# Head 0's keys and queries loaded earlier from a pool of their own, and the second layer's input transposed through more PSUM banks

## The chip, the cores and the metric

The kernel is one program for one core of a Trainium2 chip. Its engines are TensorE (PE, matmul; PEld is its weight load), VectorE (DVE), ScalarE (ACT), GpSimd (POOL) and SyncE (SP), which issues the DMAs here. Each engine works through its own list of instructions in order, so an instruction that waits holds up all behind it on that engine. The metric is the device time of one execution, in microseconds (us).

## The reference

Two layers over 512 latent tokens of width 2048, with 256 context tokens. Layer 1: modulated RMSNorm, one input projection, then a gated MLP (groups of 128 channels mixed over chunks of 128 tokens) and differential attention of 8 heads, concatenated, projected and added. Layer 2: modulated RMSNorm, projection into a, b and g, depthwise convolution of 31 taps, LayerNorm, gate, output projection.

```python
# even layer (layer 1)
q, k = diff_qk(bq, ...), diff_qk(bk, ...)      # RMSNorm per head, axial rotary on latents
p = softmax(q0 k0 / 8) - lam * softmax(q1 k1 / 8)
ob = p @ v                                     # keys and values: 512 latent + 256 context
ya = u * (w_s @ rms_norm(v) + b_s) * silu(ag)
yb = rms_norm(ob) * (1 - lambda_init) * silu(bg)
x1 = x + gt * (concat(ya, yb) @ w_out)
# odd layer (layer 2)
h2 = modulate(rms_norm(x1), shift, scale)
a, b, g = split(h2 @ w_in)
y = silu(layer_norm(conv31(a * sigmoid(b)))) * silu(g)
out = x1 + gt2 * (y @ w_out)
```

All is float32. The kernel splits each matmul operand into two reduced-precision parts, hi and lo, and adds three products, so a logical matmul is three matmul instructions.

## The kernel before

Weights stream from HBM in blocks of 1 MB (`load_w`): a DMA into one of three `raw` buffers (line 95), a cast on ScalarE to `whi` (line 103), a subtraction on VectorE or GpSimd to `wlo` (line 104); `whi` and `wlo` have two buffers each. The order of most work is set by a scheduler that models the time when the program is built; in the attention stage the order on TensorE is written out by hand (`manual_schedule`). Where a tile pool takes memory that an earlier pool has given back, the first use waits for the last users of that memory.

The stages that matter, in order of time:

- Queries, until about 478 us: `m_block` computes Q, `qk_post` normalises, rotates (tables `CG`, `SG`), transposes and splits it, and stores it to scratch in HBM (`q_s`, line 565). Pool group `p12a` closes behind it.
- AV, about 470 to 550 us: projection of the gating values, 4 weight blocks for each of two column halves. At its start SyncE loads the gating bias `bsb` and the mixing weights `wsr` (lines 654, 659). In each block's hook a block of another matrix (`raw<-in_o_ada_w_dram`) is loaded and added on VectorE into `acc` (lines 464, 466), for the second layer's modulation; these share the three `raw` buffers with the weights. VectorE also scales `bsb` (line 655).
- U, about 550 to 652 us: `t_group` for two groups of 4 column tiles, gating on VectorE (`mx`, line 711), stores to `ug_s`.
- Attention, 652 to about 970 us: pools `psS`, `psT`, `psO` and `at` open. For each head `load_kq` loads keys and queries in four DMAs: `kk` twice (384 KB each) and `qq` twice (512 KB each), all into 64 partitions; `load_v` loads values. TensorE fills its time with the projections of the two gates (`fill`, tiles `fm`), three matmuls a unit. It runs 24 units (FP), then `scores` of head 0's first query tile (`S`), 8 more units, then the rhythm of scores, transposes of weights, values and fill. `scores` writes one buffer `S` (3 banks); its maxima (line 855) and exponentials (line 865) must have read it before the next scores.
- Output projection and second layer's input, about 970 to 1190 us: `x1_done` and `x1_last` make x1, `make_h2` transposes it in halves of 256 tokens: for two k-tiles at a time, 4 matmuls with the identity into one bank `z` from `psM` (2 banks), then ScalarE writes `h2h` (line 1061) and VectorE `h2l` (line 1062). `t_half_steps` multiplies the halves with the first weights of the second layer (banks `a01` from `psA4`, 6 banks); after it come another `t_half` and the groups `tg`.
- The second layer, to the end: TensorE runs without gaps.

Of the kernel before, what the change touches and what calls it, by code (L numbers as in the profile page):

```python
# [11 lines left out]
F32 = mybir.dt.float32  # L12
F32R = mybir.dt.float32r
# [6 lines left out]
P = 128  # L20
D = 2048
KT = D // P
T = 512
# [3 lines left out]
TA = T + TC  # L27
# [3 lines left out]
DH = 64  # L31
# [14 lines left out]
def hybrid_layers_kernel(  # L46
# [7 lines left out]
    V, A, G, PE, SP = nc.vector, nc.scalar, nc.gpsimd, nc.tensor, nc.sync  # L54
# [7 lines left out]
    def nm(s):  # L62
        uid[0] += 1
        return f"{s}_{uid[0]}"

    def mm(o, l, r, start, stop):
        return PE.matmul(o, l, r, start=start, stop=stop)  # L67
# [7 lines left out]
    def htile(s, dt=F32R):  # L75
        return hp.tile([P, T], dt, tag="h", name=nm(s))

    def dscr(shape, s):
        return dr.tile(shape, F32, name=s, tag=s)
# [7 lines left out]
    q_s = dscr([H, 2, P, T], "q_s")  # L87
    k_s = dscr([H, 2, P, TA], "k_s")
# [26 lines left out]
    def t_group(W, c0, mov, pool, tag, ntile=4, nk=4, lo_eng=None, hook=None, prologue=None):  # L115
        ncols = ntile * P
        ps = [pool.tile([P, T], F32, tag=tag, name=nm("tg")) for _ in range(ntile)]
        for gi in range(KT // nk):
            hi, lo = load_w(W, gi * nk * P, nk, c0, ncols, lo_eng)
            for j in range(ntile):  # L120
                for k in range(nk):
                    kt = gi * nk + k
                    mh, ml = mov[kt]
                    wh, wl = hi[:, k, j * P : (j + 1) * P], lo[:, k, j * P : (j + 1) * P]
                    mm(ps[j], wh, mh, kt == 0, False)
                    mm(ps[j], wl, mh, False, False)
                    mm(ps[j], wh, ml, False, kt == KT - 1)
            if hook:
                hook(gi)
        return ps  # L130
# [95 lines left out]
    p123 = ctx.enter_context(ExitStack())  # L226
# [3 lines left out]
    def zt(n=T):  # L230
        return psM.tile([P, n], F32, tag="m", name=nm("z"))
# [415 lines left out]
    p12a.close()  # L647


    p12b = p12.enter_context(ExitStack())  # L650
    bp = p12b.enter_context(tc.tile_pool(name="bp", bufs=2))
    c2 = p12b.enter_context(tc.tile_pool(name="c2", bufs=1))
# [40 lines left out]
    for ug in range(2):  # L693
        ps = t_group(e_w_in, C_U + 512 * ug, hm, psA, "m", hook=u_hook if ug == 0 else hook2)
        for j in range(4):
            g = 4 * ug + j
            gu = bp.tile([P, T], F32, tag="gu", bufs=3, name=nm("gu"))
            A.activation(gu, ps[j], AF.Gelu)
            z = zt()
            for n in range(NT):  # L700
                o_ = z[:, n * P : (n + 1) * P]
                vh, vl = vn[n][0][:, g * P : (g + 1) * P], vn[n][1][:, g * P : (g + 1) * P]
                mm(o_, vh, wsh[:, g, :], True, False)
                mm(o_, vh, wsl[:, g, :], False, False)
                mm(o_, vl, wsh[:, g, :], False, True)
            z3 = z.rearrange("p (n q) -> p n q", q=P)
            V.scalar_tensor_tensor(
                z3, z3, gvh[:, g : g + 1], bsb[:, g, :].unsqueeze(1).broadcast_to([P, NT, P]), op0=ALU.mult, op1=ALU.add,
            )
            mx = bp.tile([P, T], F32, tag="mx", name=nm("mx"))  # L710
            V.tensor_tensor(mx, z, gu, op=ALU.mult)  # L711
            SP.dma_start(ug_s[g], mx)
    p12.close()


# [4 lines left out]
    at = p3.enter_context(tc.tile_pool(name="at", bufs=2))  # L720
# [96 lines left out]
    def fill(n):  # L817
        while n > 0 and not held:
            r = next(fs, None)
            if r != "more":  # L820
                held.append(r)
            n -= 1

    KQ, VV, S0, OT, PP = {}, {}, {}, {}, {}

    def load_kq(h):
        kk = at.tile([P, 2, TA], F32R, tag="kk", bufs=2, name=nm("kk"))
        qq = at.tile([P, 4, T], F32R, tag="qq", bufs=2, name=nm("qq"))
        for s in range(2):
            ds_ = slice(DH * s, DH * s + DH)  # L830
            SP.dma_start(kk[ds_].bitcast(F32), k_s[h, s].rearrange("(m d) t -> d m t", d=DH))
        for s in range(2):
            ds_ = slice(DH * s, DH * s + DH)
            SP.dma_start(qq[ds_].bitcast(F32), q_s[h].rearrange("s (m d) t -> d (s m) t", d=DH))
        KQ[h] = ([kk[:, m, :] for m in range(2)], [[qq[:, 2 * s + m, :] for s in range(2)] for m in range(2)])

    def load_v(h):
        vv = at.tile([P, 12, P], F32R, tag="vv", bufs=1, name=nm("vv"))
        SP.dma_start(vv.bitcast(F32), v_s[h].rearrange("s (k p) d -> p (s k) d", p=P))
        VV[h] = (vv[:, 0:6], vv[:, 6:12])  # L840
# [3 lines left out]
    def scores(h, qt):  # L844
        KK, QQ = KQ[h]
        if qt == 0:
            S0[h] = at.tile([P, NT], F32, tag="s0", name=nm("s0"))
        Sx = psS.tile([P, 2, TA], F32, tag="s", name=nm("S"))
        for m in (1, 0):
            for i, qx in enumerate(QQ[m]):  # L850
                for r0, r1 in (((0, 512), (512, 768)) if m == 0 else ((0, 256), (256, 768))):
                    mm(Sx[:, m, r0:r1], qx[:, qt * P : (qt + 1) * P], KK[m][:, r0:r1], i == 0, i == 1)
        mx = at.tile([P, 2], F32, tag="mx", name=nm("mx"))
        for m in (1, 0):
            V.reduce_max(mx[:, m : m + 1], Sx[:, m, :], axis=AX.X, negate=True)
        EX[h, qt] = (Sx, mx)
# [70 lines left out]

    with tc.manual_schedule(engines={mybir.EngineType.PE}):
        units = [(h, qt) for h in range(H) for qt in range(NT)]
        load_kq(0)  # L930
        load_v(0)
        fill(FP)
        scores(*units[0])
        weights(*units[0])
        fill(32 - FP)
        norm, outp = None, None
        for u, (h, qt) in enumerate(units):
            tail = u >= 4 * H - 4
            f0, f1, f2 = (2, 2, 2) if tail else (F0, F1, 8 - F0 - F1)
            if qt == 0 and h + 1 < H:  # L940
                load_kq(h + 1)
            if u + 1 < len(units):
                scores(*units[u + 1])
            fill(f0)
            turn(h, qt)
            if u + 1 < len(units):
                weights(*units[u + 1])
            fill(f1)
            if norm:
                outp = norm()  # L950
                norm = None
            if qt % 2:
                values(h, qt // 2)
                if outp:
                    outp()
                    outp = None
                if qt == 3:
                    norm = head_sums(h)
                    if h + 1 < H:
                        load_v(h + 1)  # L960
            fill(f2)
        outp = norm()
        fill(99)
        outp()
        for _ in fs:
            pass


    p3.close()
    psA = ctx.enter_context(tc.tile_pool(name="psA4", bufs=6, space=PSUM))  # L970
    rs4 = ctx.enter_context(tc.tile_pool(name="rs4", bufs=16))
    sg4 = ctx.enter_context(tc.tile_pool(name="sg4", bufs=12))
# [2 lines left out]
    def z4(n=T):  # L975
        return psM.tile([P, n], F32, tag="m", name=nm("z4"))

    def mt():
        return psA.tile([P, T], F32, tag="m", name=nm("m4"))
# [65 lines left out]

    def make_h2(half, kts):
        ts_ = slice(256 * half, 256 * half + 256)
        for k0 in range(kts[0], kts[1], 2):
            z = z4()
            for i in range(2):  # L1050
                for u in range(2):
                    kt, t = k0 + i, 2 * half + u
                    PE.transpose(z[:, 256 * i + u * P : 256 * i + (u + 1) * P],
                                 x1[t][kt // 4][:, (kt % 4) * P : (kt % 4 + 1) * P], ident)
            for i in range(2):
                kt = k0 + i
                if len(h2) <= kt:
                    h2.append((htile("h2h"), htile("h2l")))
                hi, lo = h2[kt]
                z_ = z[:, 256 * i : 256 * i + 256]  # L1060
                A.activation(hi[:, ts_], z_, AF.Identity, bias=sh2[:, kt : kt + 1])
                V.scalar_tensor_tensor(lo[:, ts_], z_, sh2[:, kt : kt + 1], hi[:, ts_].bitcast(F32), op0=ALU.add, op1=ALU.subtract)
# [39 lines left out]
    for t in range(2, NT):  # L1102
        part(t, 0)
    make_h2(0, (0, 8))
    for t in range(2, NT):
        part(t, 1)
        x1_last(t, ps[t][:, 0:256])
    make_h2(0, (8, 16))
    while ada_tail:
        ada_step(z4)  # L1110
# [112 lines left out]
    for i in range(KT):  # L1223
        if y2m[i] is None:
            z = z4()
# [61 lines left out]
```

## Time and profile before

| | |
|---|---|
| median of 3 runs | 1850.77 us (1850.75 to 1851.95) |
| profiled execution | 1853.68 us, span 1851.9 us |
| TensorE busy | 1805.9 us, 98% of the span, 8767 matmuls |
| VectorE busy | 1122.3 us (61%) |
| ScalarE busy | 559.8 us (30%) |
| GpSimd busy | 446.9 us (24%) |
| mean granted clock of TensorE | 0.996 of 2.4 GHz |
| DMA | 327.34 MB, mean 177 GB/s |

Read the span first, then the share of TensorE. It has little idle time, so what matters are the places where it waits or runs at the lower clock; the list of waits gives them, and the timelines of the engine that it waits for tell why. Lengths of matmuls in a timeline overlap, since they are pipelined: the distance between two starts is what one costs.

### The profile page before, as it was taken

How to read it: one execution, taken by the hardware profiler on the slowest of the kernel's cores; microseconds unless marked ns; L12 is line 12 of the kernel's file. 1: busy time of each engine (PE TensorE's matmuls, PEld its weight loads, DVE VectorE, ACT ScalarE, POOL GpSimd, SP SyncE). 2: the span in 40 equal slices, each digit the busy share in tenths (PEclk: the TensorE clock that was granted, in tenths of full speed). 3: DMA queues.
4: the chain of work that ended last, by engine and by line, in shares of the span. 5: the costliest groups of instructions: out<-in, count | busy, mean ns of one | idle time of the engine just before them, and what ended most of it. 6: DMA issues, size and time to landing. Idle time of an engine off the chain costs nothing.

```text
span 1851.9 us, 21931 instructions
## 1 busy us (share of the span) xinstructions
PE 1805.9 (98%) x8767; PEld 1475.8 (80%) x8767; DVE 1122.3 (61%) x1571; ACT 559.8 (30%) x747; POOL 446.9 (24%) x173
## 2 busy tenths in 40 slices
PE   5899999999999989999999999999999999999998
PEld 2557888888878878888888889888888888888887
DVE  4438546288556336666674555149999999765111
ACT  3322212222323124444442225322222222464120
POOL 0002002011000032232310002245445544444332
PEclk9999999999999999999999999999999999999999
DMA  9997764397767485655656772222332233224441
GB/s 312 360 333 254 245 240 123 118 347 232 241 230 240 165 225 161 170 164 167 203 193 228 250 232 86 91 91 91 102 103 91 91 104 101 91 91 142 149 158 52
DMA packets 208487, 327.34 MB, mean 177 GB/s; under 512 B 10249, under 2 KB 116610, under 8 KB 200194
## 3 DMA queue, kind: packets, MB, share of 16 engines
q1 hardware_dynamic: 208386, 325.94, 54.5%
q8 instruction: 69, 1.13, 0.3%
q14 instruction: 32, 0.26, 0.0%
HBM read 292.33 MB, written 33.58 MB: 176 GB/s over the span
## 4 chain that ended last, share of the span: by engine, by line
PE 83%; DMA 8%; DVE 4%; issue 2%; ACT 1%; POOL 1%; SPq 1%; DVEq 0%; ACTq 0%; POOLq 0%
PE tg L67 31%; PE mb L67 20%; PE m L67 14%; PE fm L67 8%; DMA raw<-in_o_ada_w_dram 3%; PE S L67 2%; PE oT L67 2%; PE z L305 2%; DVE wlo L104 2%; DVE acc L466 1%; DMA raw<-in_e_w_in_dram 1%; PE t L883 1%; DMA qq<-q_s 1%; DMA x_s<-x 1%; POOL wlo L104 1%
## 5 line engine op out<-in xcount | busy, mean ns | idle before, releaser
L104 POOL TENSOR_TENSOR wlo<-raw,whi 128x2048 fp32r<-128x2048 f32 x80 | 369.3, 4617 | 634.1 <-ACT whi L103 626.7
L103 ACT CAST whi<-raw 128x2048 fp32r<-128x2048 f32 x136 | 259.6, 1909 | 697.3 <-PE tg L67 209.7
L1152 DVE SCALAR_TENSOR_TENSOR z<-y,dwc,z 128x512 f32<-128x512 f32 x480 | 319.4, 749 | 0.1
L67 PE MATMUL tg<-h2h,wlo 128*128 128x512 f32 x704 | 274.7, 390 | 0.0
L67 PE MATMUL tg<-h2l,whi 128*128 128x512 f32 x704 | 273.9, 389 | 0.0
L67 PE MATMUL tg<-h2h,whi 128*128 128x512 f32 x704 | 270.8, 389 | 0.0
L67 PE MATMUL mb<-whi,hhi 128*128 128x512 f32 x512 | 203.0, 398 | 1.4 <-DVE ms L193 1.4
L67 PE MATMUL mb<-wlo,hhi 128*128 128x512 f32 x512 | 201.1, 393 | 1.5 <-DVE wlo L104 1.3
L104 DVE TENSOR_TENSOR wlo<-raw,whi 128x2048 fp32r<-128x2048 f32 x56 | 128.2, 2290 | 120.4 <-ACT whi L103 120.1
L67 PE MATMUL mb<-whi,hlo 128*128 128x512 f32 x512 | 200.9, 392 | 0.0
L466 DVE SCALAR_TENSOR_TENSOR acc<-raw,silu_c,acc 128x2048 f32<-128x2048 f32 x60 | 141.0, 2351 | 91.1 <-DMA raw<-in_o_ada_w_dram 70.2
L67 PEld LDWEIGHTS tg<-h2l,whi 128*128 128x128 f32 x704 | 132.2, 188 | 27.8 <-issue 0.5
L67 PEld LDWEIGHTS tg<-h2h,wlo 128*128 128x128 f32 x704 | 132.2, 188 | 27.7 <-issue 0.5
L67 PEld LDWEIGHTS tg<-h2h,whi 128*128 128x128 f32 x704 | 132.2, 188 | 27.5
L194 POOL TENSOR_TENSOR rs<-ms,mhalf 128x8 f32<-128x8 f32 x20 | 35.5, 1784 | 377.8 <-DVE ms L193 377.8
L67 PEld LDWEIGHTS mb<-whi,hhi 128*128 128x128 f32 x512 | 96.5, 189 | 34.6 <-issue 13.5
L67 PEld LDWEIGHTS mb<-wlo,hhi 128*128 128x128 f32 x512 | 96.7, 189 | 21.7 <-DVE wlo L104 2.7
L67 PEld LDWEIGHTS mb<-whi,hlo 128*128 128x128 f32 x512 | 96.6, 189 | 20.3
L67 PE MATMUL fm<-hhi,whi 128*128 128x512 f32 x256 | 106.7, 417 | 0.6 <-DVE mx L711 0.6
L67 PE MATMUL fm<-hlo,whi 128*128 128x512 f32 x256 | 101.1, 395 | 0.0
L67 PE MATMUL fm<-hhi,wlo 128*128 128x512 f32 x256 | 100.8, 394 | 0.0
L67 PE MATMUL m<-wlo,y2h 128*128 128x512 f32 x256 | 99.6, 389 | 0.0
(260 smaller groups left out, 3004.4 us busy)
## 6 DMA issues: line engine op xcount, KB each, us to landing
raw<-in_e_w_in_dram SPq DMA_DIRECT2D x56, 1024.0 KB, 6.4
raw<-in_o_ada_w_dram SPq DMA_DIRECT2D x48, 1024.0 KB, 5.0
raw<-in_o_w_in_dram SPq DMA_DIRECT2D x48, 1024.0 KB, 5.1
raw<-in_e_ada_w_dram SPq DMA_DIRECT2D x64, 512.0 KB, 7.2
raw<-in_e_ada_w_dram SPq DMA_DIRECT2D x16, 1024.0 KB, 6.7
raw<-in_e_w_out_dram SPq DMA_DIRECT2D x16, 1024.0 KB, 5.2
raw<-in_o_w_out_dram SPq DMA_DIRECT2D x16, 1024.0 KB, 5.0
qq<-q_s SPq DMA_DIRECT2D x16, 512.0 KB, 11.9
```

What stands on the lines that cost most here:

```text
L67: return PE.matmul(o, l, r, start=start, stop=stop)
L103: A.copy(hi, raw)
L104: (lo_eng or V).tensor_tensor(lo, raw, hi.bitcast(F32), op=ALU.subtract)
L194: G.tensor_tensor(dst, tmp, mhalf[:, 0:1].broadcast_to([P, n]), op=ALU.pow)
L305: PE.matmul(ada_ps[j][32 * g : 32 * g + 32, 0 : 2 * nc_], S[:, kt, :], raw[:, i, :], start=(kt < 4), stop=(kt >= KT - 4), skip_group_check ...
L466: V.scalar_tensor_tensor(ada_state["acc"], raw, sc_[:, jt : jt + 1], ada_state["acc"], op0=ALU.mult, op1=ALU.add)
L883: PE.transpose(z[:, k * P : (k + 1) * P], e[:, (k0 + k) * P : (k0 + k + 1) * P], ident)
L1152: V.scalar_tensor_tensor(zi if t == TAPS - 1 else z, y2[:, t : t + T], w(t), z, op0=ALU.mult, op1=ALU.add)
```

## The change

There are two edits. First, `load_kq` is defined before the AV stage and takes its tiles for even heads from a new pool `kq0`, opened where `p12a` has closed; odd heads use pool `at`, each with one buffer where `at` had two. Head 0's load is called after the first U group instead of at the start of attention. Second, `make_h2` takes every other transpose bank from `psA4` (`mt()`) instead of `psM` (`z4()`).

```diff
--- before.py
+++ after.py
@@ -647,6 +647,23 @@
     p12a.close()
 
 
+    pkq = p123.enter_context(ExitStack())
+    kq0 = pkq.enter_context(tc.tile_pool(name="kq0", bufs=1))
+    KQ = {}
+
+    def load_kq(h):
+        pool = at if h % 2 else kq0
+        kk = pool.tile([P, 2, TA], F32R, tag="kk", bufs=1, name=nm("kk"))
+        qq = pool.tile([P, 4, T], F32R, tag="qq", bufs=1, name=nm("qq"))
+        for s in range(2):
+            ds_ = slice(DH * s, DH * s + DH)
+            SP.dma_start(kk[ds_].bitcast(F32), k_s[h, s].rearrange("(m d) t -> d m t", d=DH))
+        for s in range(2):
+            ds_ = slice(DH * s, DH * s + DH)
+            SP.dma_start(qq[ds_].bitcast(F32), q_s[h].rearrange("s (m d) t -> d (s m) t", d=DH))
+        KQ[h] = ([kk[:, m, :] for m in range(2)], [[qq[:, 2 * s + m, :] for s in range(2)] for m in range(2)])
+
+
     p12b = p12.enter_context(ExitStack())
     bp = p12b.enter_context(tc.tile_pool(name="bp", bufs=2))
     c2 = p12b.enter_context(tc.tile_pool(name="c2", bufs=1))
@@ -710,6 +727,8 @@
             mx = bp.tile([P, T], F32, tag="mx", name=nm("mx"))
             V.tensor_tensor(mx, z, gu, op=ALU.mult)
             SP.dma_start(ug_s[g], mx)
+        if ug == 0:
+            load_kq(0)
     p12.close()
 
 
@@ -821,18 +840,7 @@
                 held.append(r)
             n -= 1
 
-    KQ, VV, S0, OT, PP = {}, {}, {}, {}, {}
-
-    def load_kq(h):
-        kk = at.tile([P, 2, TA], F32R, tag="kk", bufs=2, name=nm("kk"))
-        qq = at.tile([P, 4, T], F32R, tag="qq", bufs=2, name=nm("qq"))
-        for s in range(2):
-            ds_ = slice(DH * s, DH * s + DH)
-            SP.dma_start(kk[ds_].bitcast(F32), k_s[h, s].rearrange("(m d) t -> d m t", d=DH))
-        for s in range(2):
-            ds_ = slice(DH * s, DH * s + DH)
-            SP.dma_start(qq[ds_].bitcast(F32), q_s[h].rearrange("s (m d) t -> d (s m) t", d=DH))
-        KQ[h] = ([kk[:, m, :] for m in range(2)], [[qq[:, 2 * s + m, :] for s in range(2)] for m in range(2)])
+    VV, S0, OT, PP = {}, {}, {}, {}
 
     def load_v(h):
         vv = at.tile([P, 12, P], F32R, tag="vv", bufs=1, name=nm("vv"))
@@ -927,7 +935,6 @@
 
     with tc.manual_schedule(engines={mybir.EngineType.PE}):
         units = [(h, qt) for h in range(H) for qt in range(NT)]
-        load_kq(0)
         load_v(0)
         fill(FP)
         scores(*units[0])
@@ -967,6 +974,7 @@
 
 
     p3.close()
+    pkq.close()
     psA = ctx.enter_context(tc.tile_pool(name="psA4", bufs=6, space=PSUM))
     rs4 = ctx.enter_context(tc.tile_pool(name="rs4", bufs=16))
     sg4 = ctx.enter_context(tc.tile_pool(name="sg4", bufs=12))
@@ -1045,8 +1053,8 @@
 
     def make_h2(half, kts):
         ts_ = slice(256 * half, 256 * half + 256)
-        for k0 in range(kts[0], kts[1], 2):
-            z = z4()
+        for n, k0 in enumerate(range(kts[0], kts[1], 2)):
+            z = mt() if n % 2 else z4()
             for i in range(2):
                 for u in range(2):
                     kt, t = k0 + i, 2 * half + u
```

The scheduler decides where the instructions land. On SyncE, at the end of the query stores, the kernel before has these rows (`q_s` stores, then `bsb`, `wsr` and the streams of weights and modulation):

```order
L565 DMA q_s<-qklo_3350 128x4x128
L565 DMA q_s<-qkhi_3374 128x4x128
L95 DMA raw_3619<-in_e_w_in_dram 128x4x512
L565 DMA q_s<-qklo_3375 128x4x128
L565 DMA q_s<-qkhi_3399 128x4x128
L565 DMA q_s<-qklo_3400 128x4x128
L654 DMA bsb<-in_e_a_bs_dram 128x1024
L659 DMA wsr<-in_e_a_ws_dram 128x8x128
L95 DMA raw_3673<-in_o_ada_w_dram 128x2048
L95 DMA raw_3692<-in_e_w_in_dram 128x4x512
```

and the changed kernel these, in the same place:

```order
L565 DMA q_s<-qklo_3350 128x4x128
L660 DMA kk_4297<-k_s 64x2x768 x2
L663 DMA qq_4298<-q_s 64x4x512
L565 DMA q_s<-qkhi_3374 128x4x128
L663 DMA qq_4298<-q_s 64x4x512
L95 DMA raw_3622<-in_e_w_in_dram 128x4x512
L565 DMA q_s<-qklo_3375 128x4x128
L565 DMA q_s<-qkhi_3399 128x4x128
L565 DMA q_s<-qklo_3400 128x4x128
L671 DMA bsb<-in_e_a_bs_dram 128x1024
L676 DMA wsr<-in_e_a_ws_dram 128x8x128
L95 DMA raw_3676<-in_o_ada_w_dram 128x2048
```

Head 0's four loads (`kk` twice, `qq` twice) now stand among the query stores, ahead of the weight block `raw_3622` and of three stores; the rest keeps its order. At the start of attention, where they stood between the last weight block of the gates and `vv`, they are gone, and nothing else on SyncE has moved there.

On VectorE, at the start of the AV stage, the kernel before has

```order
L112 TENSOR_TENSOR qklo_3400<-z_3394,qkhi_3399 128x512
L655 TENSOR_SCALAR bsb<-bsb 128x1024
L104 TENSOR_TENSOR wlo_3622<-raw_3619,whi_3621 128x2048
L514 TENSOR_TENSOR A_96<-z_3546,o_b_92 128x16
L464 TENSOR_SCALAR acc_3555<-raw_3553,silu_c 128x2048
L516 TENSOR_TENSOR A_96<-A_96,g_89 128x16
L466 SCALAR_TENSOR_TENSOR acc_3555<-raw_3616,silu_c,acc_3555 128x2048
```

and the changed one

```order
L112 TENSOR_TENSOR qklo_3400<-z_3394,qkhi_3399 128x512
L104 TENSOR_TENSOR wlo_3625<-raw_3622,whi_3624 128x2048
L514 TENSOR_TENSOR A_96<-z_3549,o_b_92 128x16
L464 TENSOR_SCALAR acc_3558<-raw_3556,silu_c 128x2048
L672 TENSOR_SCALAR bsb<-bsb 128x1024
L516 TENSOR_TENSOR A_96<-A_96,g_89 128x16
L466 SCALAR_TENSOR_TENSOR acc_3558<-raw_3619,silu_c,acc_3558 128x2048
```

The scaling of `bsb` has moved behind the split of a weight block (`wlo`) and the first modulation step (`acc`). On TensorE, the transposes of x1 come in runs of up to 12 where they came in runs of up to 6, since four banks stand open at once instead of two; there are still 16 rounds of four, more of them early. At the end of the second half, where the next weights (`whi_9124`, accumulators `m_1485`, `m_1486`) begin, the kernel before has

```order
L67 MATMUL m_1468_8841<-h2l_8803,whi_8935 128x256
L67 MATMUL m_1469_8842<-h2l_8803,whi_8935 128x256
L67 MATMUL m_1485_9120<-h2h_8659,whi_9124 128x512
L67 MATMUL m_1486_9121<-h2h_8659,whi_9124 128x512
L67 MATMUL m_1468_8841<-h2h_8806,whi_8935 128x256
L67 MATMUL m_1468_8841<-h2h_8806,wlo_8936 128x256
L67 MATMUL m_1469_8842<-h2h_8806,whi_8935 128x256
L67 MATMUL m_1469_8842<-h2h_8806,wlo_8936 128x256
L67 MATMUL m_1485_9120<-h2h_8659,wlo_9125 128x512
L67 MATMUL m_1485_9120<-h2l_8660,whi_9124 128x512
L67 MATMUL m_1485_9120<-h2h_8663,whi_9124 128x512
```

with 26 matmuls of the earlier accumulators `m_1468`, `m_1469` and 4 transposes still to come behind these rows, and the changed one

```order
L67 MATMUL m_1469_8846<-h2h_8836,wlo_8940 128x256
L67 MATMUL m_1469_8846<-h2l_8837,whi_8939 128x256
L67 MATMUL m_1485_9124<-h2h_8663,whi_9128 128x512
L67 MATMUL m_1486_9125<-h2h_8663,whi_9128 128x512
L67 MATMUL m_1485_9124<-h2h_8663,wlo_9129 128x512
L67 MATMUL m_1485_9124<-h2l_8664,whi_9128 128x512
L67 MATMUL m_1485_9124<-h2h_8667,whi_9128 128x512
```

where all of those stand ahead of the first `m_1485`. The instructions on each engine are the same in number, and from here to the end their order is the same as before.

## Rows read from the trace of the kernel before

**Rows 1.** TensorE timeline, 672 to 684 us: start, length, instruction, count, idle before.
```profile
672.63 2.90 PE L67 MATMUL S<-kk,qq 128*128 128x256 f32 x8 [3.75 <-DMA qq<-q_s]
...
675.33 0.63 PE L67 MATMUL fm<-hhi,whi 128*128 128x512 f32 x1
...
682.36 1.57 PE L67 MATMUL S<-kk,qq 128*128 128x256 f32 x8
```

**Rows 2.** Stretch: length, busy PE, PEld, DVE, ACT, POOL, granted clock, DMA share, GB/s.
```profile
672.60:678.60 6.00, 5.97 (x16) 4.93 (x17) 1.82 (x2) 1.13 (x1) 0.00 (x0) 0.50 1.05 232
```

**Rows 3.** TensorE timeline, 490 to 540 us.
```profile
493.35 0.27 PE L524 MATMUL z<-ident,A 128*16 128x128 f32 x1
...
527.59 0.50 PE L67 MATMUL mb<-wlo,hhi 128*128 128x512 f32 x1 [1.06 <-DVE wlo L104]
...
539.04 0.50 PE L67 MATMUL mb<-wlo,hhi 128*128 128x512 f32 x1 [0.28 <-DVE wlo L104]
```

**Rows 4.** TensorE timeline, 1129 to 1192 us: all its waits there.
```profile
1145.22 0.39 PE L67 MATMUL m<-h2h,whi 128*128 128x256 f32 x1 [0.53 <-ACT h2h L1061]
...
1164.65 0.50 PE L67 MATMUL m<-h2h,wlo 128*128 128x512 f32 x1 [0.92 <-DVE wlo L104]
...
1180.70 0.50 PE L67 MATMUL m<-h2h,wlo 128*128 128x512 f32 x1 [1.25 <-DVE wlo L104]
```

**Rows 5.** SyncE's queue, 657 to 670 us: issue start, length, line, transfer, count.
```profile
657.84 1.32 SPq L831 DMA_DIRECT2D kk<-k_s  x2
659.20 1.86 SPq L834 DMA_DIRECT2D qq<-q_s  x2
...
661.75 7.88 SPq L831 DMA_DIRECT2D kk<-k_s  x2
```

**Rows 6.** Chain of waits, 680 to 692 us: start, length, what.
```profile
685.96 4.12 PE fm L67 x18
```

**Rows 7.** Timelines of VectorE and ScalarE, 675 to 681 us.
```profile
675.57 1.82 DVE L855 TENSOR_REDUCE mx<-S 128x1 f32<-128x768 f32 x2 [5.33 <-PE S L67]
...
679.66 0.89 ACT L865 ACTIVATE e<-S,mx 128x768 f32<-128x768 f32 x1
```

**Rows 8.** SyncE's queue, 468 to 491 us.
```profile
468.82 0.36 SPq L565 DMA_DIRECT2D q_s<-qklo  x1
...
472.86 0.37 SPq L95 DMA_DIRECT2D raw<-in_e_w_in_dram  x1
...
476.56 0.36 SPq L565 DMA_DIRECT2D q_s<-qklo  x1
481.40 0.35 SPq L654 DMA_DIRECT2D bsb<-in_e_a_bs_dram  x1
...
490.56 0.37 SPq L95 DMA_DIRECT2D raw<-in_e_w_in_dram  x1
```

**Rows 9.** Stretches as in rows 2: a later head's loads; the query stores.
```profile
702.60:711.00 8.40, 8.40 (x47) 7.11 (x46) 6.24 (x12) 3.56 (x8) 3.91 (x1) 1.00 1.02 228
470.00:480.00 10.00, 10.00 (x52) 7.35 (x51) 3.71 (x4) 2.18 (x4) 0.00 (x0) 1.00 0.78 228
```

**Rows 10.** Timelines of ScalarE and VectorE, 480 to 504 us.
```profile
481.71 1.91 ACT L103 CAST whi<-raw 128x2048 fp32r<-128x2048 f32 x1 [2.33 <-PE mb L67]
...
486.36 0.70 DVE L655 TENSOR_SCALAR bsb<-bsb 128x1024 f32<-128x1024 f32 x1 [9.83 <-DMA bsb<-in_e_a_bs_dram]
486.97 2.28 DVE L104 TENSOR_TENSOR wlo<-raw,whi 128x2048 fp32r<-128x2048 f32 x1
...
500.86 2.29 DVE L104 TENSOR_TENSOR wlo<-raw,whi 128x2048 fp32r<-128x2048 f32 x1 [3.92 <-ACT whi L103]
```

**Rows 11.** VectorE timeline, 1160 to 1166 us.
```profile
1162.31 2.29 DVE L104 TENSOR_TENSOR wlo<-raw,whi 128x2048 fp32r<-128x2048 f32 x1 [1.31 <-ACT whi L103]
```

**Rows 12.** TensorE timeline at the start: transposes of x.
```profile
30.18 1.53 PE L345 MATMUL xz<-ident,x 128*128 128x128 f32 x12
```

**Rows 13.** The stretch around rows 12, columns as in rows 2.
```profile
28.00:32.00 4.00, 4.00 (x26) 1.63 (x20) 4.00 (x8) 0.00 (x0) 0.00 (x0) 1.00 1.10 348
```

## The prediction

> **What bounds the kernel now.** I read the list of TensorE's waits first, then the timeline around each larger one, then the timelines of the engines it waited for. TensorE has little idle time, so the change can only win where TensorE waits or runs at the lower clock, and it touches three such places.
>
> The first is the start of attention. TensorE stands 3.75 us until head 0's queries have landed, and the first scores then run slowly: the same 8 matmuls take 2.90 us there and 1.57 us one query tile later [rows 1]. The stretch after the wait shows a granted clock of 0.50, that is 1.2 of 2.4 GHz [rows 2]. The second is the AV stage, with two waits for `wlo`, 1.06 and 0.28 us [rows 3]. The third is the stretch where the second layer's input is transposed: three waits, 0.53, 0.92 and 1.25 us [rows 4].
>
> **Head 0's loads at the start of attention.** SyncE issues them at 657.84 and 659.20 [rows 5]. In the changed order they stand some 190 us earlier, so the scores follow the 24 fill units at 672.63 - 3.75 = 668.88 us. Three sums go. The wait: 3.75. The scores: 2.90 - 1.57 = 1.33. The 24 matmuls behind them took 682.36 - 675.33 = 7.03 us [rows 1]; at the full clock 18 take 4.12 us [rows 6], so 24 take 5.49, a gain of 1.54. Together 6.6 us.
>
> What is late next? The second scores write the buffer that the exponentials of the first must have read. From the end of the first scores (the maxima start at 675.57) to the end of the last exponential (679.66 + 0.89) it is 4.98 us [rows 7]. In the changed kernel the first scores end at 668.88 + 1.57 = 670.45, the exponentials at 675.43, and TensorE is through its 24 matmuls at about 670.45 + 5.49 - 0.2 = 675.7. That hides the chain with 0.3 us to spare; I count nothing, with 0.3 as the worse bound. The other loads there (`vv`, head 1's) leave the queue earlier than before.
>
> **The loads in their new place.** They come behind the store issued at 468.82 [rows 8]. Four issues cost 1.32 + 1.86 = 3.2 us on SyncE [rows 5], so SyncE is through them by about 472.4 and the weight block of 472.86 [rows 8] is not issued late. The DMA engines are another matter. Four loads carry 1.835 MB; where a later head's loads run alone, the stretch moves 228 GB/s with the engines full, so they take 8.0 us. In the ten microseconds of the query stores the engines are 0.78 busy, so 2.2 us of that fits [rows 9], and 5.8 us push what stands behind: the weight block, three stores, and `bsb`, which waits for the last store and goes from 481.40 to 487.2.
>
> Does TensorE feel it? The weight block had landed before its cast at 481.71, which waited for TensorE to release the buffer [rows 10]. Pushed by 5.8 it lands at 487.5 at the latest; cast 1.91 and split 2.28 [rows 10] give 491.7, and TensorE changes to that block at about 493.35 [rows 3]: hidden, with 1.6 to spare. This needs the split not to stand behind `bsb` on VectorE; before, it did (486.36, then 486.97 [rows 10]), and the new order has it ahead. `bsb` itself lands 4.96 us after its issue (481.40 to 486.36), so it is scaled at 492.2 to 492.9. The modulation column behind it is what the small transpose at 493.35 on TensorE reads [rows 3]: 0.4 to spare.
>
> The split ends up to 2.4 us later than before (491.7 against 486.97 + 2.28 = 489.25), and that delay runs on: the three `raw` buffers pass from weights to modulation blocks and back, and a block is issued only when VectorE has read the one before, as that of 490.56 [rows 8]. Its split ended at 503.15 [rows 10]; TensorE, after 48 more matmuls of 0.229 us, wants it at 504.3. 1.2 of the 2.4 us are hidden there. At 527.59, where TensorE already waits, nothing is. So the price lies between 1.2 and 2.4; I take 1.8. The bounds: a gain of 1.3, if the block comes no later and the split, now free of `bsb`, ends earlier, so that both waits [rows 3] go; a loss of 5.8, if the whole push reaches TensorE.
>
> For comparison, and nothing else rests on it: the Trainium skill (SBUF — State Buffer, Door 1: The DMA port swizzle) says that a transfer into 64 partitions reaches only half of the ports and measures 196 GB/s for one of 1 MiB. By that the loads would take 9.4 us (an estimate) and push 7.2 instead of 5.8. The 228 GB/s of rows 9 are a little better, and decide.
>
> **The transposes.** Same instructions, so only the waits can go: 0.53 + 0.92 + 1.25 = 2.70 [rows 4]. The first is for `h2h`, written by ScalarE behind a scaling of x1; with four banks open more of `h2h` is written ahead of that scaling. The second arises because TensorE stands at the new weights' `wlo` (ready at 1162.31 + 2.29 = 1164.60 [rows 11]) with 26 older matmuls and 4 transposes still behind it. In the new order those 30 stand ahead; at 0.13 us each, the length of a transpose [rows 12], they are 3.8 us of work, and cover 0.92. The third is the same one block on: its buffer came free only when those 30 were done, and now it does so before the block of 48 matmuls of 512 columns starts. ScalarE's cast now stands behind all the `h2h`, but those need the transposes, which are all issued 3 us or more before TensorE leaves that cast's buffer. I take 2.7; the other bound is no gain, if the longer runs only move the waits.
>
> **Sum.** -6.6 + 1.8 - 2.7 = -7.5 us. The profiled execution took 1853.68 us, its span and 1.8 around it; it would take 1846.2. The runs' median is 1850.77, 2.9 lower, so I forecast 1843.3 there. Less than 0.2%, 3.7 us, can't be told from no change.
>
> **Rivals.**
> - The push reaches TensorE whole: +5.8 instead of +1.8, so -3.5 and 1847.3. For it: VectorE works in order, `bsb` stands in the middle of it, and an issue of loads once held SyncE 7.88 us with much in flight (661.75 [rows 5]). Against: there the load followed five others, here mostly stores.
> - The AV stage gains: -6.6 - 1.3 - 2.7 = -10.6, 1840.2. For it: the split of the first block is free of `bsb`. Against: the engines are full for 8 us more.
> - Something else is late at 668.88 and only the wait goes: -3.75 + 1.8 - 2.7 = -4.7, 1846.1. The exponentials are the nearest, by 0.3 us.
> - The change does not do what it says at the transposes, since ScalarE and VectorE write no faster: -4.8, 1846.0.
> - Slower: runs of 12 transposes let the clock fall, as the wait at 668.88 did. From the first transposes to the 512-column matmuls it is 35 us; at half rate +35, 1878. It decides once more than 7.5 us of that work is done at half rate. Against: 12 transposes in a row at 30.18 [rows 12] lie in a stretch granted 1.00 [rows 13]. For comparison: the Trainium skill (TensorE: Matmul & The Clock Gate, Part 4: PE-mode transpose) says that a transpose does not count as TensorE being busy in the same way; by that rule this rival would be likely, and rows 13 disagree.
>
> **Chances and range.** Forecast 0.64, push 0.13, AV gain 0.12, only the wait 0.05, no gain at the transposes 0.03, clock 0.03. The unknown ends alone give 1840.2 (all gains) to 1850.3 (-6.3 + 5.8 and no gain at the transposes); 1839.5 to 1848.0 leaves out the clock and the double misfortune. Faster by over 0.2%, below 1847.1: the forecast, the AV gain and the two small rivals, 0.84. Within: 0.13, the push. Slower: 0.03.
>
> **What would show it.** In the new profile: no wait of `S` for `qq`, the first scores in about 1.6 us, and the granted clock at 1.00 in that stretch. `bsb` issued about 487, and TensorE's waits for `wlo` between 500 and 540 summing to some 3 us where they were 1.3. None of the three waits between 1130 and 1192. Wrong: a wait of several microseconds at the small transpose or at a `wlo` before 505, a granted clock under 1.00 among the transposes, or second scores that wait for the exponentials.

## The result, and the profile after

The changed kernel took 1843.3 us (median of 1841.36, 1843.35 and 1843.3), beside 1850.77 for the kernel before: a ratio of 0.9948 with a 95% interval of 0.9928 to 0.9968. Two later comparisons, with more runs, gave 0.9945 (0.9930 to 0.9960) and 0.9941 (0.9927 to 0.9954). The forecast time, 1843.3, was hit, and the two medians of this first comparison differ by the forecast 7.5 us, a ratio of 0.9960. With more runs the difference is larger: the medians of the two later comparisons differ by 10.9 and 12.0 us, and on 1851 us the three ratios are -9.6, -10.2 and -10.9 us. The interval of the first still holds 0.9960, that of the second ends there, and that of the third leaves it out.

The profiled execution took 1841.36 us, span 1839.6, TensorE busy 1799.3 us.

First the start of attention. TensorE's timeline (start, length, instruction, count), to be read against [rows 1]:

```profile
666.51 1.57 PE L67 MATMUL S<-kk,qq 128*128 128x256 f32 x8
...
673.40 1.56 PE L67 MATMUL S<-kk,qq 128*128 128x256 f32 x8
```

and the stretch behind it (length, busy PE, PEld, DVE, ACT, POOL, granted clock, DMA share, GB/s), against [rows 2]:

```profile
666.50:672.50 6.00, 6.00 (x30) 4.98 (x29) 2.67 (x4) 3.07 (x5) 1.40 (x1) 1.00 1.07 220
```

No wait stands in brackets, the scores take 1.57 us at once, and the granted clock is 1.00 where it was 0.50. ScalarE ends the exponentials of these scores here:

```profile
672.20 0.89 ACT L873 ACTIVATE e<-S,mx 128x768 f32<-128x768 f32 x1
```

That is 673.09, and the second scores start at 673.40: the chain has 0.3 us to spare, against [rows 7].

Second the AV stage. SyncE's queue (issue start, length, transfer), against [rows 8]:

```profile
468.37 1.33 SPq L660 DMA_DIRECT2D kk<-k_s  x2
469.74 0.61 SPq L663 DMA_DIRECT2D qq<-q_s  x1
...
471.72 0.92 SPq L95 DMA_DIRECT2D raw<-in_e_w_in_dram  x1
...
484.65 0.35 SPq L671 DMA_DIRECT2D bsb<-in_e_a_bs_dram  x1
...
488.01 0.37 SPq L95 DMA_DIRECT2D raw<-in_e_w_in_dram  x1
```

ScalarE and VectorE, against [rows 10]:

```profile
482.48 1.90 ACT L103 CAST whi<-raw 128x2048 fp32r<-128x2048 f32 x1 [4.29 <-DMA raw<-in_e_w_in_dram]
484.42 2.29 DVE L104 TENSOR_TENSOR wlo<-raw,whi 128x2048 fp32r<-128x2048 f32 x1 [9.07 <-ACT whi L103]
...
488.81 0.69 DVE L672 TENSOR_SCALAR bsb<-bsb 128x1024 f32<-128x1024 f32 x1 [0.82 <-DMA bsb<-in_e_a_bs_dram]
```

and TensorE's only wait there, against [rows 3]:

```profile
526.00 0.50 PE L67 MATMUL mb<-wlo,hhi 128*128 128x512 f32 x1 [0.67 <-DVE wlo L104]
```

The load does push: `bsb` is issued 3.3 us later by the clock (4.4 us later counted from the same `q_s` store in both, at 468.04 and 466.86), and the cast at 482.48 waits for its block where it waited for TensorE before. But the split ends at 486.71, and before it ended at 489.25, since it no longer stands behind `bsb`. One wait is left of two.

Third the transposes. The whole stretch from the first transpose to the first `tg`, in the kernel before and after:

```profile
1129.50:1191.30 61.80, 59.10 (x404) 53.96 (x403) 23.83 (x49) 28.25 (x48) 15.21 (x13) 1.00 0.28 90
```
```profile
1121.30:1179.00 57.70, 57.70 (x404) 53.93 (x404) 23.03 (x49) 28.01 (x48) 15.26 (x13) 1.00 0.29 94
```

The same 404 instructions take 4.1 us less: the 2.70 us of idle time of [rows 4] are gone, and the busy time fell by 1.40 as well. The granted clock is 1.00, with transposes in a row as here:

```profile
1128.85 0.60 PE L1061 MATMUL z<-ident,x 128*128 128x128 f32 x4
1129.29 1.04 PE L1061 MATMUL m<-ident,x 128*128 128x128 f32 x8
```

Something else got worse. In the output projection, which the change does not touch, a wait stands in both kernels, before and after:

```profile
1077.51 0.50 PE L67 MATMUL m<-wlo,yh 128*128 128x512 f32 x1 [0.58 <-DVE wlo L104]
```
```profile
1069.47 0.50 PE L67 MATMUL m<-wlo,yh 128*128 128x512 f32 x1 [1.53 <-DVE wlo L104]
```

To compare executions stage by stage I set marks: the `q_s<-qkhi` store near 468 ("the mark" below), the first `tg<-hhi` (end of AV), the first `fm`, the first `S`, the first `m<-whi,yh`, the first `tg<-h2h`. The table holds the distances, in us, for the traces of before, of after and of the experiments below; the last column lists TensorE's waits for `wlo` between the last two marks, first those in the output projection, and behind a semicolon those among the transposes.

| trace | store at | AV | fm to S | S to m | m to tg | waits for wlo |
|---|---|---|---|---|---|---|
| before | 468.0 | 81.8 | 20.3 | 304.4 | 214.2 | 0.58; 0.92, 1.25 |
| after | 466.9 | 80.8 | 16.4 | 301.5 | 210.9 | 1.53 |
| r_after | 464.9 | 80.6 | 16.4 | 301.5 | 213.7 | 1.34, 2.40 |
| r2_after | 465.6 | 80.8 | 16.4 | 301.4 | 210.4 | 0.96 |
| e1_load | 466.9 | 80.4 | 16.5 | 301.6 | 214.3 | 0.73; 0.93, 1.26 |
| e2_banks | 467.2 | 82.9 | 21.2 | 304.4 | 211.0 | 1.53 |
| e4_bsb | 466.3 | 79.9 | 22.4 | 303.1 | 214.3 | 0.42; 0.93, 1.26 |
| e9_double | 467.9 | 81.7 | 16.4 | 301.5 | 211.1 | 1.67 |
| e7_behind_bsb | 467.3 | 82.4 | 16.4 | 301.9 | 209.6 | 0.17 |
| e3_hold | 467.4 | 79.9 | 18.0 | 301.6 | 209.7 | 0.20 |
| e5_hold_bsb | 465.3 | 79.9 | 16.4 | 301.5 | 209.4 | 0 |
| e5b_hold_bsb | 465.3 | 79.9 | 16.4 | 301.3 | 211.3 | 1.86 |
| e6_allmt | 468.4 | 80.9 | 16.4 | 301.2 | 210.0 | 0 |

Before minus after, stage by stage: the start, which no edit touches, 1.2; AV 1.0; `fm` to the first scores 3.9; the scores and the matmuls behind them 2.9; the last stage 3.3, that is 4.2 from the transposes less 0.95 lost in the projection. Together that is the 12.3 us between the two spans.

### The profile page after: what moved, and what is told of

Read it like the earlier page. It is cut to its first block, busy times and chain, and to the rows that moved or that the text cites. A ratio compares the mean times of both kernels' runs of the same rounds, so it can differ in the third digit from the quotient of the medians.

```text
span 1839.6 us, 21926 instructions
## 1 busy us (share of the span) xinstructions
PE 1799.3 (98%) x8767; PEld 1473.0 (80%) x8767; DVE 1120.9 (61%) x1571; ACT 559.8 (30%) x747; POOL 447.3 (24%) x173
## 4 chain that ended last, share of the span: by engine, by line
PE 83%; DMA 8%; DVE 4%; issue 2%; POOL 1%; SPq 1%; ACT 1%; DVEq 0%; ACTq 0%; POOLq 0%
PE tg L67 31%; PE mb L67 19%; PE m L67 15%; PE fm L67 9%; DMA raw<-in_o_ada_w_dram 4%; PE S L67 2%; PE oT L67 2%; PE z L305 2%; DVE wlo L104 1%; DVE acc L466 1%; DMA raw<-in_e_ada_w_dram 1%; PE t L891 1%; DMA x<-in_x_dram 1%; POOL wlo L104 1%; DMA raw<-in_e_w_in_dram 0%
## 5 line engine op out<-in xcount | busy, mean ns | idle before, releaser
L103 ACT CAST whi<-raw 128x2048 fp32r<-128x2048 f32 x136 | 259.7, 1910 | 709.2 <-PE tg L67 209.4
```

The source lines that it names most:

```text
L103: A.copy(hi, raw)
```

## The experiments

**The changed kernel again (r_after, r2_after).** No edit. First:

> The changed kernel once more, for a tighter ratio and a second trace. Against before, the two traces so far differ by 12.3 us, of which 1.2 arise at the start of the program, which the change does not touch; the medians differ by 7.5. Theory (three places gain: AV stage 1.0, start of attention 6.8, transposes 4.3, and a wait for a weight block in the output projection, 0.58 before and 1.53 after, takes 0.95 back by chance): a difference of 9 to 12 us in the medians here. Rival (the sum of the forecast, with the AV stage 1.8 worse, is right, and the trace was a lucky one): 7 to 8 us, and a trace with two or more waits for wlo between 500 and 550.

Then, beside the last two experiments:

> The changed kernel a third time, as the measure for the two that run beside it. Theory: a ratio of 0.993 to 0.996 again, and an AV stage (from the qkhi store near 468 to the first matmul tg) of 80 to 81 us, where the kernel before took 81.9 and 82.9 in two traces. Rival (the gain in the AV stage was chance): 82 us or more there.

Measured: 1842.54 beside 1853.44 (10.9 us between the medians, 10.2 by the ratio) and 1839.18 beside 1851.22 (12.0 and 10.9). AV took 80.6 and 80.8 us. The theory of 9 to 12 us holds, and the forecast's sum falls. The start differs by 2 us between these executions of one program, and the waits in the projection by 2.8, so a single median of three can be off by the 3 us that made the forecast look exact.

**The load alone (e1_load).**

```diff
-        for n, k0 in enumerate(range(kts[0], kts[1], 2)):
-            z = mt() if n % 2 else z4()
+        for k0 in range(kts[0], kts[1], 2):
+            z = z4()
```

> The pool and the early load alone; make_h2 as before. Theory: -7 to -8 us (start of attention -6.8, AV stage -1.0), and the three waits at the transposes are back, 2.7 us of idle time. Rival 1 (the banks give nothing in the time, since the waits only move): the same as the changed kernel within 1 us. Rival 2 (the load costs 1.8 in the AV stage): -4.8.

Measured: 1844.98, ratio 0.9959 (0.9944 to 0.9973), -7.6 us. TensorE's waits at the transposes:

```profile
1136.48 0.39 PE L67 MATMUL m<-h2h,whi 128*128 128x256 f32 x1 [0.50 <-ACT h2h L1069]
...
1155.93 0.50 PE L67 MATMUL m<-h2h,wlo 128*128 128x512 f32 x1 [0.93 <-DVE wlo L104]
...
1171.97 0.50 PE L67 MATMUL m<-h2h,wlo 128*128 128x512 f32 x1 [1.26 <-DVE wlo L104]
```

These are the three of [rows 4], within 0.03 us. The theory holds, and rival 2 (-4.8) is outside the interval. Rival 1 is not excluded by the times alone, since the intervals overlap; the table excludes it, with 214.3 us from `m` to `tg` as before.

**The banks alone (e2_banks).** The same two lines, put into the kernel before.

> The transposes through both pools alone; keys and queries as before. Theory: -4.3 us, more than the 2.7 of the three listed waits, because stalls below 0.1 us that the list does not show go too; no wait between the first transpose and the first tg. Rival 1 (only the listed waits go): -2.7. Rival 2 (longer runs of transposes give nothing or let the clock fall): 0 or slower, with a granted clock under 1.00 there.

Measured: 1849.33, ratio 0.9977 (0.9967 to 0.9988), -4.3 us. The stretch of the transposes:

```profile
1132.00:1189.60 57.60, 57.60 (x403) 53.86 (x402) 23.05 (x49) 27.98 (x48) 15.28 (x13) 1.00 0.29 94
```

Nothing waits, the clock is 1.00, and 57.6 us compare with 57.7 in the changed kernel and 61.8 in the two without the edit. Theory: -4.3 met. Within the intervals the two edits add up: -7.6 and -4.3 against the -10 to -11 of both. The part that has no row in the list of waits is 1.4 us of busy time; where within the 404 instructions it arises stays open. TensorE's waits in the unchanged AV stage of this execution were

```profile
527.58 0.50 PE L67 MATMUL mb<-wlo,hhi 128*128 128x512 f32 x1 [1.87 <-DVE wlo L104]
539.30 0.50 PE L67 MATMUL mb<-wlo,hhi 128*128 128x512 f32 x1 [0.53 <-DVE wlo L104]
```

where the kernel before, with the same order of instructions up to here, waited 1.06 and 0.28: these waits scatter by themselves.

**The load held until U (e3_hold).**

```diff
-            SP.dma_start(ug_s[g], mx)
+            ug_st = SP.dma_start(ug_s[g], mx)
         if ug == 0:
-            load_kq(0)
+            with tc.issue_after(ug_st.ins):
+                load_kq(0)
```

> The changed kernel, with head 0's load held until the first U group's stores have been issued, so that nothing is pushed in the query stores; the scaling of bsb stands ahead of the weight block's split again, as before. Theory (the AV stage gained because the split no longer waited behind bsb): the AV stage goes back to two waits for wlo, 1.06 and 0.28, the kernel is 0.5 to 1.0 us slower than the changed one, and the start of attention keeps its gain. Rival (the early load costs something in the AV stage, as forecast, and the gain there was chance): 1 to 2 us faster than the changed kernel.

Measured: 1841.01, ratio 0.9937 (0.9921 to 0.9953). It is not slower, and AV took 79.9 us without any wait for `wlo`, although `bsb` is scaled ahead of the split again. The two waits that the theory wanted are not there. The rival's 1 to 2 us lie where the intervals overlap, and stay unproved. The trace shows something that was not looked for. TensorE's first gate matmul, and the stretch around it:

```profile
650.52 0.47 PE L67 MATMUL fm<-hhi,whi 128*128 128x512 f32 x1 [1.00 <-DVE mx L728]
```
```profile
648.00:656.00 8.00, 7.00 (x30) 5.77 (x30) 2.81 (x4) 0.60 (x2) 6.27 (x2) 0.79 0.69 224
```

After 1.00 us of waiting (and 0.40 us four microseconds earlier) the granted clock averages 0.79 over these 8 us, and `fm` to the first scores takes 18.0 us instead of 16.4. In the changed kernel the same two waits, in order of time, are 0.39 and 0.54 us, and the clock stays at 1.00. So the time of this version holds a loss of its own, and says little about the AV stage.

**The order of `bsb` and split without the load (e4_bsb).** On SyncE `wsr` goes ahead of `bsb` here as well, which it does not in the changed kernel.

```diff
-    SP.dma_start(bsb, e_a_bs[0].partition_broadcast(P))
-    V.tensor_scalar(bsb, bsb, 0.5, None, op0=ALU.mult)
 ...
         ps = m_block(e_w_in, C_AV + 512 * hb, lat(), psA, "m", hook)
 ...
+    SP.dma_start(bsb, e_a_bs[0].partition_broadcast(P))
+    V.tensor_scalar(bsb, bsb, 0.5, None, op0=ALU.mult)
```

> The kernel before, with bsb's load and scaling written behind the AV blocks, so that on VectorE the weight block's split goes ahead of the scaling, as in the changed kernel, and on SyncE wsr goes ahead of bsb; no early load, transposes as before. In the traces so far the next weight block is issued 22.5, 22.0 and 21.6 us after the qkhi store at 468 where bsb is scaled first, and 21.2, 21.3 and 21.1 us after it where the split is first. Theory (that swap is what offset the early load's push): 20 to 21 us here, without the push, and -0.5 to -1.0 us of time, below what the ratio can show. Rival (the swap is nothing; the waits for wlo of 0 to 2.4 us in this stage come from how late a block lands after its issue): 21.6 to 22.5 us, and waits in that range.

Measured: 1853.35 beside 1853.56, ratio 1.0000 (0.9985 to 1.0014). VectorE, SyncE and the first scores:

```profile
481.94 2.29 DVE L104 TENSOR_TENSOR wlo<-raw,whi 128x2048 fp32r<-128x2048 f32 x1 [7.13 <-ACT whi L103]
485.23 0.69 DVE L676 TENSOR_SCALAR bsb<-bsb 128x1024 f32<-128x1024 f32 x1 [0.99 <-DMA bsb<-in_e_a_bs_dram]
```
```profile
487.23 0.38 SPq L95 DMA_DIRECT2D raw<-in_e_w_in_dram  x1
```
```profile
670.71 2.90 PE L67 MATMUL S<-kk,qq 128*128 128x256 f32 x8 [5.76 <-DMA qq<-q_s]
```

The next block is issued 20.9 us after the mark, in the theory's 20 to 21, and AV takes 79.9 us without a wait, 2.0 less than before. (e3_hold took as little with `bsb` scaled first, so one pair of traces does not show that the order did it.) The time does not show the 2.0, and the last row tells why: TensorE comes to the first scores 2 us earlier, and waits 5.76 us for the queries instead of 3.75. Here the gain ahead of a wait for a transfer went into that wait.

**Load held, and split first (e5_hold_bsb, e5b_hold_bsb).** Both edits above on the changed kernel, measured twice.

> The changed kernel, with head 0's load held behind the first U group's stores and bsb's load and scaling behind the AV blocks: no push, and the split ahead of the scaling. Theory (the early load costs the AV stage some of what the swap gives): 1 to 2 us faster than the changed kernel's ratio of 0.9945, that is 0.9935 to 0.9940, and no wait for wlo in the AV stage. Rival (neither matters, the stage's waits are chance): 0.9945, and the wait for wlo at about 525 is 0.4 to 2 us again.

> The kernel with the held load and bsb's scaling behind the split, again, beside the changed one. Theory (it takes the load out of the AV stage and keeps the split free of bsb, so that nothing in that stage waits): an AV stage of 79.8 us, and 1 to 3 us less than the changed kernel on the same chip, ratio 0.9915 to 0.9935 to before. Rival (the difference of the first try, 0.9926 to 0.9945, was scatter): the same ratio as the changed kernel within 0.0005.

Measured: 0.9926 (0.9905 to 0.9946), then 0.9937 (0.9923 to 0.9951) beside 0.9941 for the changed kernel on the same chip. AV took 79.9 us twice, without a listed wait of over 0.2. So the stage is some 0.9 us shorter than in the changed kernel, as the theory has it, but the 1 to 3 us of the second theory did not come: the time cannot tell the two apart, 1839.19 and 1839.18, and the ratios differ by 0.0004, as its rival has it. The wait of 1.86 us in the projection, in the second try, is larger than that gain. Whether this version beats the changed kernel stays open.

**The load behind `bsb` (e7_behind_bsb).**

```diff
-    SP.dma_start(bsb, e_a_bs[0].partition_broadcast(P))
+    bsb_ld = SP.dma_start(bsb, e_a_bs[0].partition_broadcast(P))
 ...
         if ug == 0:
-            load_kq(0)
+            with tc.issue_after(bsb_ld.ins):
+                load_kq(0)
```

> The changed kernel, with head 0's load issued right behind bsb and wsr, about 12 us later than in the changed kernel; bsb's scaling is ahead of the split again. Theory (the forecast's own rule: loads that stand ahead of weight blocks delay them, and about 1.2 us of that is hidden): the blocks behind land 3 to 4 us later, TensorE waits 2 to 3 us for wlo at about 504, and the ratio is 0.995 to 0.997. Rival (SyncE stands idle there, since the next blocks wait for their buffers, so that the load fills a gap): no wait of over 1 us before 515, ratio 0.994 to 0.995.

Measured: 1844.35, ratio 0.9954 (0.9936 to 0.9973). ScalarE and TensorE:

```profile
501.98 1.91 ACT L103 CAST whi<-raw 128x2048 fp32r<-128x2048 f32 x1 [19.13 <-DMA raw<-in_e_w_in_dram]
```
```profile
506.27 0.50 PE L67 MATMUL mb<-wlo,hhi 128*128 128x512 f32 x1 [1.83 <-DVE wlo L104]
```

The block issued at 488.96 is cast 13.0 us later (8.4 us in the kernel before, from 490.56 to 498.92), and TensorE waits 1.83 us for its split. AV takes 82.4 us, 1.6 more than in the changed kernel. Theory: met, nearly in size. That this place is dearer than the one among the stores is only in part shown, since `bsb` and the split have changed places too. With `bsb` first and no load in the stage the same block is cast 30.9, 31.9 and 29.0 us behind the mark (before, e2_banks, e3_hold), and here 34.7: that lateness is more than scatter. But AV took 81.8, 82.9 and 79.9 us in those three, so 82.4 is no loss beyond scatter.

**The early load doubled (e9_double).**

```diff
         if ug == 0:
             load_kq(0)
+            with tc.issue_after(last_qq[0].ins):
+                SP.dma_start(dscr([2, P, TA], "k_copy"), k_s[0])
+                for i in range(2):
+                    SP.dma_start(dscr([2, P, T], f"q_copy{i}"), q_s[0])
```

> The changed kernel with the early load's bytes doubled: behind head 0's loads come copies of 0.75, 0.5 and 0.5 MB from scratch to scratch in HBM, which nothing reads. Theory (a push is felt once it exceeds the stage's slack): bsb is issued 7 to 8 us later than in the changed kernel, the weight blocks land 3 to 5 us later, TensorE waits 2 to 4 us for a wlo before 515, and the time is 2 to 4 us above the changed kernel's. Rival (the stage swallows such loads, since its blocks are paced by their buffers and not by the DMA engines): within 1 us of it, and no wait of over 1 us before 515.

Measured: 1840.09, ratio 0.9928 (0.9905 to 0.9951). SyncE, VectorE and TensorE:

```profile
489.88 0.35 SPq L672 DMA_DIRECT2D bsb<-in_e_a_bs_dram  x1
```
```profile
487.00 2.29 DVE L104 TENSOR_TENSOR wlo<-raw,whi 128x2048 fp32r<-128x2048 f32 x1 [10.60 <-ACT whi L103]
```
```profile
504.53 1.20 PE L67 MATMUL mb<-whi,hhi 128*128 128x512 f32 x4
505.56 0.73 PE L681 MATMUL z<-ident,wsr 128*128 128x128 f32 x5
506.86 0.50 PE L67 MATMUL mb<-wlo,hhi 128*128 128x512 f32 x1 [0.57 <-DVE wlo L104]
```

In its time and its wait the theory falls; the rival's condition on the waits is met, and by the ratios (0.9945 and 0.9941 for the changed kernel) the time is no longer. From the mark, `bsb` is issued 4.2 us later than in the changed kernel (21.96 against 17.79), not 7 to 8; the split of the first block ends at 489.29, where the kernel before has 489.25; and TensorE waits 0.57 us. AV grows by 0.8 us, and U, from which some of the small transposes of `wsr` have moved into AV, gives 0.6 of it back (101.8 us against 102.4).

But the stage does not swallow the bytes. The second weight block, in this kernel and in the changed one:

```profile
502.57 1.91 ACT L103 CAST whi<-raw 128x2048 fp32r<-128x2048 f32 x1 [3.59 <-DMA raw<-in_e_w_in_dram]
```
```profile
497.06 1.91 ACT L103 CAST whi<-raw 128x2048 fp32r<-128x2048 f32 x1 [12.68 <-DMA raw<-in_e_w_in_dram]
```

It is cast 34.7 us behind the mark against 30.2: 4.4 us later, inside the theory's 3 to 5, and as late as in e7_behind_bsb (34.7). There TensorE waited 1.83 us for the split; here the order on TensorE has changed too, and four matmuls that need only `whi` and transposes of `wsr` stand in the gap (rows above). So twice the bytes cost next to nothing in time because other work covered most of the late block.

**All transposes in one pool (e6_allmt).**

```diff
-            z = mt() if n % 2 else z4()
+            z = mt()
```

> The changed kernel with all transposes of the second layer's input in banks of psA4 (6 banks, shared with the accumulators) and none in psM. Theory (with two banks of each pool nothing waits any more, so more banks of one pool can add nothing): the same time within 1 us and no wait between the first transpose and the first tg, unless the accumulators need those banks; then a wait of m or a01 of up to 1 us. Rival (the number of open banks is still what limits): 1 to 2 us faster than the changed kernel, since the stalls too short for the list go as well.

Measured: 1841.86, ratio 0.9955 (0.9940 to 0.9971), the changed kernel beside it 0.9941. TensorE's one wait there:

```profile
1131.13 0.36 PE L67 MATMUL m<-h2h,whi 128*128 128x256 f32 x1 [0.72 <-DVE xl L1028]
```

As the theory allowed: the accumulators share these banks, and one waits 0.72 us until x1's last columns are read out. More banks of the one pool gain nothing; from `m` to `tg` it takes 210.0 us with that wait in it, where the other kernels with the edit take 209.4 to 209.9 once their waits in the projection are taken off.

## Why the prediction was right, and where it was not

- **Start of attention, -6.6: right in each step.** From `fm` to the first scores 3.9 us went (3.75 forecast), from the first to the second scores 9.73 - 6.89 = 2.84 (1.33 + 1.54 = 2.87). The exponentials keep the 0.3 us that the prediction worked out. In e1_load, -7.6 us with the AV gain in it, it stands alone.
- **AV stage, +1.8: the failed step, by sign.** The step was: "Pushed by 5.8 it lands at 487.5 at the latest; cast 1.91 and split 2.28 [rows 10] give 491.7". The block was cast at 482.48 and split by 486.71. Two things were mis-sized. The 5.8 was laid whole on a cast that, by the prediction's own reading, had waited for TensorE and not for its block; 491.7 was thus the latest end of the split, and the 1.8 was worked out from it as if it were the likely one. Counted from the mark the cast came 1.9 us later than before (15.6 against 13.7) and `bsb` 4.4 later. Also, the free room was counted over the ten microseconds of [rows 9], and behind the stores there is more: over 23 us from about the mark the kernel before has a DMA share of 0.60, which leaves 9.2 us for the 8.0 of the load, and the changed one 0.87 (stretches as above, of before and of after):

```profile
467.00:490.00 23.00, 23.00 (x115) 18.19 (x114) 9.88 (x12) 6.09 (x6) 0.00 (x0) 1.00 0.60 170
```
```profile
465.80:488.80 23.00, 23.00 (x115) 18.19 (x114) 9.81 (x12) 6.08 (x6) 0.00 (x0) 1.00 0.87 238
```

  And the new order on VectorE was used as cover for the push, not as a gain of its own. With it the split ended 19.9 us behind the mark, not later than before (21.2) but earlier, so the delay that was to run on to the next blocks never arose: the second block's split ended 34.4 us behind the mark, before 35.1. How much the order gives and the push takes is known only in part. With the split first AV takes 79.9 us in the three traces without the load (e4_bsb, e5_hold_bsb, e5b_hold_bsb) and 80.4 to 80.9 in five with it, so the push takes 0.5 to 1.0, if the place of `wsr`, ahead of `bsb` in those three, does nothing. With `bsb` first and no load in the stage it took 79.9, 81.8 and 82.9, so that the order gives anything from 0 to 3 us. The measured term is -1.0, near the rival with -1.3 that had 0.12; it is no larger than this scatter, and shown is only that the loss of 1.8 did not come.
- **Transposes, -2.7: right mechanism, too small.** The three waits went in every kernel with the edit and stayed in every one without. The stretch gained 4.1 to 4.2, because busy time fell too, by 1.4. The prediction put that part at nothing ("only the waits can go"); where in the stretch it arises stays open.
- **Sum.** By the traces -6.8 - 1.0 - 4.2 = -12.0, of which the wait in the projection took 0.95 back: -11.1 for the profiled pair, and -9.6 to -10.9 by the ratios. Errors of 2.8 and 1.5 us in one direction, and scatter of the first comparison's medians of some 3 us in the other, gave the forecast its exact time: that was luck.
- **Rivals.** No whole push, no late exponentials, no fallen clock: granted 1.00 in both stretches. The Trainium skill (TensorE: Matmul & The Clock Gate, Part 4: PE-mode transpose) says that a transpose does not count as TensorE being busy in the same way; the stretch with 64 transposes in runs of up to 12, at 1.00 throughout, does not bear out a loss from it here. By the Trainium skill's figure for a transfer into 64 partitions (SBUF — State Buffer, Door 1: The DMA port swizzle) the push would have been larger, 7.2 us by the prediction's estimate; `bsb` came 4.4 us later, counted from the mark. The estimate does not fit these loads: of each pair one goes into partitions 0 to 63 and the other into 64 to 127 (`ds_` in `load_kq`), so the figure for one such transfer is no bound on the four together.

## What to carry to other kernels

Ask of a load that is moved how late it makes each block behind it, and how much that block has to spare, and do not add its whole push to one row. The second weight block of the AV stage shows the scale: its split ended 30.3 us behind the mark in e4_bsb, 34.4 in the changed kernel, and 38.9 in e7_behind_bsb and e9_double, and by the prediction's sum TensorE wants it at 36.3 (504.3 - 468.0). Only in the last two did TensorE wait there, and in one of these other work covered most of it. The free room of the stretch around the load helps to guess the lateness, but no run here tested that as a rule. When a change takes an instruction out of the way of another, give that its own term in the sum, and do not spend it as cover. And look at what stands behind the gain: what e4_bsb won went into the next wait for a transfer, which the early load takes away.

## What the runs showed that was not expected

- A wait of 1.00 us, 4 us behind one of 0.40, was followed by a mean granted clock of 0.79 over 8 us (e3_hold, one trace); waits of 0.39 and 0.54 us in the same places of the changed kernel were not.
- The same weight block, with the same order on all queues ahead of it, was cast 8.4 us after its issue in one execution (490.56 to 498.92) and 9.9 us in another (489.24 to 499.15, e2_banks). The waits in the projection lay between 0 and 3.7 us in all, and between 1.0 and 3.7 in three executions of the changed kernel; that scatter of this kind is their cause was not followed up.
- With `load_kq(0)` left at its old place in the code, but with tiles from the new pool, the scheduler puts the instructions of every engine in the same order as in the changed kernel: it is the pool's memory that lets the load go early, not the place of the call. That version was built and not run.
